# The second FFN product by seven block products for 32 of 44 tiles, between the next part's up-products

## The chip, the cores and the metric

The kernel runs on one core of a Trainium2 chip. The metric is device time in microseconds, the median of several runs. TensorE is the matmul engine, VectorE (DVE), ScalarE (ACT) and GpSimd (POOL) work on rows of 128 partitions, and SyncE (SP) issues most of the data transfers (DMA).

## The reference, cut to what matters

One decoder layer on 256 tokens and 16 meta tokens, width 2048, all in float32. Attention and pooling come first and are not touched. The change lies in the feed-forward part:

```python
def conv_gated_ffn(h, w_up, conv_w, conv_b, w_down):
    T = h.shape[1]
    z = h @ w_up                                   # 2048 -> 2 x 5632
    zp = jnp.pad(z, ((0, 0), (CONV_WIDTH - 1, 0), (0, 0)))
    z = sum(zp[:, j:j + T] * conv_w[j] for j in range(CONV_WIDTH)) + conv_b
    a, g = jnp.split(z, 2, axis=-1)
    return (jax.nn.gelu(a) * g) @ w_down           # 5632 -> 2048
...
    h = layer_norm(ALPHA * h + mix, ln1_g[l], ln1_b[l])
    f = conv_gated_ffn(h, w_up[l], conv_w[l], conv_b[l], w_down[l])
    h = layer_norm(ALPHA * h + f, ln2_g[l], ln2_b[l])
```

## The kernel before

Every float32 product is made of three matmuls. An operand is split into a high part (a copy by ScalarE to the type float32r) and a low part (VectorE subtracts that copy), and high by high, high by low and low by high are added up in PSUM. `fetch` does this for a weight tile of 128 x 2048: one DMA of 1 MB into a raw buffer, and then for each half ScalarE's copy (line 90) and VectorE's subtraction (line 91) into a tile `whl`. There are three raw and three split buffers. All weight tiles are listed in `stream` in the order of their use, and `weights` hands out the next one after `prefetch` has emitted the fetches up to two tiles ahead.

The feed-forward part has 44 tiles of 128 hidden channels, in parts of 16, 12, 12 and 4 (`PARTS`). For each tile there are two up-products (`product`, 48 matmuls of 258 columns: the a half and the g half), a `conv` on each (line 649 on ScalarE, 650 and 651 on VectorE) and a `gate` (gelu on ScalarE, a product on VectorE at line 667, and the split into `gp` at 669 and 670). After the up-products of a part come its down tiles: a tile of the rearranged w_down holds four k-tiles by 512 columns, and each of its k-tiles meets two token halves with three matmuls of 512 columns (lines 717 to 719), 24 matmuls in all. For each of four column groups the sum in PSUM is added to the residual `y2` at line 722. The last part of 4 tiles is done token half by token half at the end (lines 745 to 769), with the second layer norm and the output.

The first four tiles (`FOLDED`) run before the first layer norm's statistics are known and are put right afterwards (`unfold`); meanwhile `normalise` makes the normalised rows. The residual is put into `y2` by 16 VectorE transposes (line 704, four for each of tiles 4 to 7) and 32 DMAs of 64 KB on SyncE's queue (`residual`, line 643, four for each of tiles 8 to 15).

Each engine works through a queue of its own in order. The framework that builds the program settles each queue's order ahead of time by priority (the order of the program) and by which instructions it reckons to be ready, so that an instruction of a later step can stand ahead of one that would have to wait.

Of the kernel before, what the change touches and what calls it, by code (L numbers as in the profile page):

```python
# [31 lines left out]
TOPK = min(256, S // 4)  # L32
FF = 5632
FT = FF // P
PARTS = (16, 12, 12, 4)
FOLDED = 4
MF = 80 + C
NE = NQ + 2
# [6 lines left out]
KW = KA + KB  # L45
STRIP = 400
G_KV, G_POOL, LN1, C_W, C_B, N_COLS = 0, 2, 10, 42, 306, 394


@with_exitstack  # L50
def tile_layer(ctx, tc, xt, w_first, w_proj, w_uk, w_uv, w_pool, w_o, w_up, w_down, cols, rows, rel_bias, onehot, out):
# [8 lines left out]
    def big():  # L60
        return pm.tile([P, 512], F32, tag="mm", name="mm")
# [14 lines left out]
    f0 = d0 = 0  # L76
    for n in PARTS:
        for f in range(f0, f0 + n):
            stream += [w_up[f], w_up[FT + f]]
        stream += [w_down[d] for d in range(d0, d0 + n)]  # L80
        f0, d0 = f0 + n, d0 + n
    spare, last = len(stream) - PARTS[-1], len(stream) - 1
    ready = {}
    state = {"next": 0, "use": 0}

    def fetch(raw, hl, src, c):
        nc.sync.dma_start(raw[:, c], src)
        mid = (c.start + c.stop) // 2
        for c in (slice(c.start, mid), slice(mid, c.stop)):
            nc.scalar.activation(hl[:, 0, c], raw[:, c], AF.Copy)  # L90
            nc.vector.tensor_tensor(hl[:, 1, c], raw[:, c], hl[:, 0, c].bitcast(F32), op=ALU.subtract)  # L91

# [3 lines left out]
    def emit(i):  # L96
        if i in ready:
            return
        if i == last:

            raw = wp.tile([P, 2048], F32, tag="wraw", name="wraw")
            nc.sync.dma_start(raw, stream[i])
            ready[i] = []
            for c in range(0, 2048, 256):
                hl = ring.tile([P, 2, 256], F32R, tag="act", name="whl_r", padded_shape=[P, 2, T])
                nc.scalar.activation(hl[:, 0, :], raw[:, c:c + 256], AF.Copy)
                nc.vector.tensor_tensor(hl[:, 1, :], raw[:, c:c + 256], hl[:, 0, :].bitcast(F32), op=ALU.subtract)
# [7 lines left out]
        fetch(raw, hl, stream[i], slice(0, 2048))  # L115
        ready[i] = hl

    def prefetch(n):
# [435 lines left out]
    output(0)  # L554
    at.close()
    fp = ctx.enter_context(tc.tile_pool(name="ffn", bufs=2))
    acc = fp.tile([P, NQ], F32, name="acc", tag="acc", bufs=1)
    s1 = fp.tile([P, NQ], F32, name="s1", bufs=1)
    s2 = fp.tile([P, NQ], F32, name="s2", bufs=1)
    rs = fp.tile([P, NQ], F32, name="rs", bufs=1)  # L560
    m2 = fp.tile([P, NQ], F32, name="m2", bufs=1)
    folded = []

    def about_k(m):

        yd = y[:, m, Q0:]
        nc.vector.tensor_tensor(yd, yd, acc, op=ALU.subtract)
        sq = fp.tile([P, NQ], F32, name="sq", tag="sq")
        nc.scalar.activation(s2 if m == 0 else sq, yd, AF.Square)
        if m == 1:  # L570
            nc.gpsimd.tensor_tensor(s1, y[:, 0, Q0:], yd, op=ALU.add)
        elif m > 1:
            nc.gpsimd.tensor_tensor(s1, s1, yd, op=ALU.add)
        if m:
            nc.gpsimd.tensor_tensor(s2, s2, sq, op=ALU.add)
        a = fp.tile([P, 2, NE], F32R, name="fold", tag="gp", bufs=18)
# [67 lines left out]

    moves = [(a, b, i) for a in range(4) for b in range(4) for i in range(2)]

    def conv(j, half_, src):
        z = fp.tile([P, S], F32, name="z", tag=f"z{half_}")
        nc.scalar.activation(z, src[:, 2:NQ], AF.Identity, bias=col(C_B, j), scale=col(C_W, 3 * j + 2))  # L649
        nc.vector.scalar_tensor_tensor(z, src[:, 1:NQ - 1], col(C_W, 3 * j + 1), z, op0=ALU.mult, op1=ALU.add)  # L650
        nc.vector.scalar_tensor_tensor(z, src[:, :S], col(C_W, 3 * j), z, op0=ALU.mult, op1=ALU.add)
        return z

    def unfold(ps):
# [5 lines left out]
        w = fp.tile([P, NQ], F32, name="w", tag="acc", bufs=1)  # L660
# [4 lines left out]
    def gate(za, zg):  # L665
        nc.scalar.activation(za, za, AF.Gelu_apprx_tanh)
        nc.vector.tensor_tensor(za, za, zg, op=ALU.mult)
        a = fp.tile([P, 2, S], F32R, name="gp", tag="gp", bufs=18, padded_shape=[P, 2, NE])
        nc.scalar.activation(a[:, 0, :], za, AF.Copy)
        nc.vector.tensor_tensor(a[:, 1, :], za, a[:, 0, :].bitcast(F32), op=ALU.subtract)  # L670
        return a


    f0 = 0
    for part, n in enumerate(PARTS):
        gated = []
        for f in range(f0, f0 + n):
            if part == len(PARTS) - 1 and f - f0 in (0, 2):
                emit((last, spare)[(f - f0) // 2])
            both = []  # L680
            for half_ in range(2):
                hl = weights()
                ps = big()
                if f < FOLDED:
                    k = 0
                    if f + half_ == 0:
                        product(ps[:, :NE], hl, P, folded, 0, NE, k1=7)
                        deviation()
                        product(ps[:, :NE], hl, P, folded, 0, NE, k0=7, k1=14)
                        deviation_rows()  # L690
                        k = 14
                    product(ps[:, :NE], hl, P, folded, 0, NE, k0=k)
                    while len(h_parts) < min(KT, 3 * (2 * f + half_ + 1)):
                        normalise(len(h_parts))
                    both.append(ps)
                else:
                    product(ps[:, :NQ], hl, P, h_parts, 0, NQ)
                    both.append(conv(half_ * FT + f, half_, ps))
            if f < FOLDED:
                both = [conv(half_ * FT + f, half_, unfold(both[half_])) for half_ in range(2)]  # L700
            gated.append(gate(*both))
            if FOLDED <= f < FOLDED + 4:
                for m in range(4 * (f - FOLDED), 4 * (f - FOLDED) + 4):
                    nc.vector.transpose(y[:, m, NM:], y[:, m, NM:])
            if FOLDED + 4 <= f and part == 0:
                for _ in range(4):
                    residual(*moves.pop(0))
        if part + 1 < len(PARTS):
            for c in range(4):
                ps = [big(), big()]  # L710
                for g in range(n // 4):
                    hl = weights()
                    for k in range(4 * g, 4 * g + 4):
                        w = slice(512 * (k - 4 * g), 512 * (k - 4 * g) + 512)
                        for i in range(2):
                            t = slice(i * P, (i + 1) * P)
                            nc.tensor.matmul(ps[i], gated[k][:, 0, t], hl[:, 0, w], start=k == 0, stop=False)  # L717
                            nc.tensor.matmul(ps[i], gated[k][:, 0, t], hl[:, 1, w], start=False, stop=False)  # L718
                            nc.tensor.matmul(ps[i], gated[k][:, 1, t], hl[:, 0, w], start=False, stop=k == n - 1)  # L719
                for i in range(2):  # L720
                    yc = y2[:, i, 512 * c:512 * c + 512]
                    nc.vector.scalar_tensor_tensor(yc, yc, 1.0 if part else ALPHA, ps[i], op0=ALU.mult, op1=ALU.add)
        f0 += n


    gb = []
    for r in range(2):
        for c in range(4):
            t = fp.tile([P, 512], F32, name="gb", tag="gp", bufs=18, padded_shape=[P, 2 * NE])
            nc.gpsimd.dma_start(t, rows[r:r + 1, 512 * c:512 * c + 512].to_broadcast([P, 512]))  # L730
            gb.append(t)
    n = PARTS[-1]
    hls = [weights(ahead=n) for _ in range(n)]
    order = [0, n - 1] + list(range(1, n - 1))
    for i in range(2):
# [98 lines left out]
```

## Time and profile before

| | us |
|---|---|
| median of 3 runs | 1080.12 (1079.86 to 1081.37) |
| the profiled execution | 1081.53 |
| its span, from first to last instruction | 1079.7 |
| TensorE busy | 1064.7 |
| VectorE busy | 712.5 |
| ScalarE busy | 524.9 |
| GpSimd busy | 100.0 |

The mean granted TensorE clock was 0.997 of full speed, and 200.17 MB were moved, at 185 GB/s in the mean. Durations of one instruction are in ns in the groups and in us in the timelines. In a timeline each row is start, duration, engine, line, operation, output from input, count, and in brackets the idle time before it with what ended it. Consecutive instructions of an engine overlap a little, so what an instruction takes from its engine is the time from its start to the next one's start. In the windows the columns are the stretch, its length, the busy time of TensorE's matmuls, its weight loads, VectorE, ScalarE and GpSimd, the granted clock, the DMA engines' busy share and GB/s.

### The profile page before, as it was taken

Reading aid. Unit: us, or ns where it says so; the run is one execution under the profiler, and the core shown is the slowest. Engines: PE = TensorE matmul, PEld = TensorE weight load, DVE = VectorE, ACT = ScalarE, POOL = GpSimd, SP = SyncE. Lnnn points to the kernel's source line nnn. Section 1 sums busy time; section 2 is a strip of 40 time slices with the busy share of each in tenths; the row PEclk is TensorE's granted clock in tenths of the full one; section 3 lists DMA queues with packets and bytes.
Section 4 is the critical chain, followed back from the end, with each engine's and each line's share of the span. In section 5 each row is a group of like instructions: output and inputs, shape, how many; then the busy total and the mean of one; then the engine's idle time right before and its main releaser. Section 6 shows DMA issues by size and latency. Waiting matters only on the chain.

```text
span 1079.7 us, 18694 instructions
## 1 busy us (share of the span) xinstructions
PE 1064.7 (99%) x7770; PEld 1008.5 (93%) x7770; DVE 712.5 (66%) x1083; ACT 524.9 (49%) x828; POOL 100.0 (9%) x131
## 2 busy tenths in 40 slices
PE   9999999999999999999999999999999999999996
PEld 8998999999999999999888999998899999988995
DVE  5879468758879975665454656655556666555757
ACT  6666446645457754454333544543344454434530
POOL 1100013126454100000000000000000000001000
PEclk9999999999999999999999999999999999999998
DMA  8756533444543686665555555555555555557712
GB/s 304 256 171 235 195 138 118 164 168 156 195 157 118 200 259 201 192 203 195 185 180 187 190 178 174 196 178 185 187 212 182 173 192 181 181 187 246 274 43 79
DMA packets 47653, 200.17 MB, mean 185 GB/s; under 512 B 20390, under 2 KB 20816, under 8 KB 25168
## 3 DMA queue, kind: packets, MB, share of 16 engines
q1 hardware_dynamic: 45872, 194.11, 53.5%
q0 software_dynamic: 1120, 3.82, 1.2%
q8 instruction: 61, 1.00, 0.4%
q10 hardware_dynamic: 576, 1.05, 0.3%
q14 instruction: 24, 0.20, 0.1%
HBM read 194.75 MB, written 2.11 MB: 182 GB/s over the span
## 4 chain that ended last, share of the span: by engine, by line
PE 92%; DVE 5%; DMA 2%; ACT 1%; issue 0%; POOL 0%; SPq 0%; ACTq 0%; DVEq 0%; POOLq 0%
PE mm L142 22%; PE mm L141 22%; PE mm L143 21%; PE mm L717 7%; PE mm L718 7%; PE mm L719 7%; DVE whl L91 1%; DMA wraw<-in_w_first 1%; DVE x L632 1%; DVE hp L636 1%; DMA wraw<-in_w_proj 1%; PE at L295 0%; PE mm L747 0%; PE mm L745 0%; PE at L296 0%
## 5 line engine op out<-in xcount | busy, mean ns | idle before, releaser
L91 DVE TENSOR_TENSOR whl<-wraw,whl 128x1024 fp32r<-128x1024 f32 x344 | 421.3, 1250 | 123.1 <-ACT whl L90 121.2
L90 ACT ACTIVATE whl<-wraw 128x1024 fp32r<-128x1024 f32 x344 | 346.7, 1050 | 174.4 <-PE mm L719 120.1
L141 PE MATMUL mm<-hp,whl 128*128 128x258 f32 x1280 | 363.7, 284 | 0.0
L142 PE MATMUL mm<-hp,whl 128*128 128x258 f32 x1280 | 363.3, 284 | 0.0
L143 PE MATMUL mm<-hp,whl 128*128 128x258 f32 x1280 | 361.1, 282 | 0.0
L143 PEld LDWEIGHTS mm<-hp,whl 128*128 128x128 f32 x1280 | 244.3, 191 | 0.0
L142 PEld LDWEIGHTS mm<-hp,whl 128*128 128x128 f32 x1280 | 244.1, 191 | 0.1
L141 PEld LDWEIGHTS mm<-hp,whl 128*128 128x128 f32 x1280 | 241.8, 189 | 0.1
L650 DVE SCALAR_TENSOR_TENSOR z<-mm,cv,z 128x256 f32<-128x256 f32 x80 | 38.7, 484 | 162.6 <-ACT z L649 162.5
L649 ACT ACTIVATE z<-mm,cv 128x256 f32<-128x256 f32 x80 | 45.1, 564 | 200.5 <-PE mm L143 200.4
L717 PE MATMUL mm<-whl,gp 128*128 128x512 f32 x320 | 126.4, 395 | 0.0
L719 PE MATMUL mm<-whl,gp 128*128 128x512 f32 x320 | 126.2, 394 | 0.0
L718 PE MATMUL mm<-whl,gp 128*128 128x512 f32 x320 | 126.2, 394 | 0.0
L141 PE MATMUL mm<-xp,whl 128*128 128x256 f32 (+5 forms) x384 | 111.1, 289 | 0.0
L143 PE MATMUL mm<-xp,whl 128*128 128x256 f32 (+5 forms) x384 | 109.1, 284 | 0.8 <-DVE whl L91 0.8
L142 PE MATMUL mm<-xp,whl 128*128 128x256 f32 (+5 forms) x384 | 109.5, 285 | 0.0
L143 PEld LDWEIGHTS mm<-xp,whl 128*128 128x128 f32 x384 | 72.5, 189 | 1.3 <-DVE whl L91 1.2
L719 PEld LDWEIGHTS mm<-whl,gp 128*128 128x128 f32 x320 | 60.1, 188 | 14.3
L141 PEld LDWEIGHTS mm<-xp,whl 128*128 128x128 f32 x384 | 72.7, 189 | 0.8 <-ACT whl L90 0.2
L717 PEld LDWEIGHTS mm<-whl,gp 128*128 128x128 f32 x320 | 60.2, 188 | 13.9
L718 PEld LDWEIGHTS mm<-whl,gp 128*128 128x128 f32 x320 | 60.1, 188 | 13.9
L142 PEld LDWEIGHTS mm<-xp,whl 128*128 128x128 f32 x384 | 72.3, 188 | 0.8 <-issue 0.5
(266 smaller groups left out, 1397.6 us busy)
## 6 DMA issues: line engine op xcount, KB each, us to landing
wraw<-in_w_up SPq DMA_DIRECT2D x88, 1024.0 KB, 5.0
wraw<-in_w_down SPq DMA_DIRECT2D x44, 1024.0 KB, 4.9
wraw<-in_w_proj SPq DMA_DIRECT2D x24, 1024.0 KB, 5.0
wraw<-in_w_o SPq DMA_DIRECT2D x16, 1024.0 KB, 4.9
wraw<-in_w_first SPq DMA_DIRECT2D x9, 304.0 KB, 6.5
x<-in_xt SPq DMA_DIRECT2D x1, 2176.0 KB, 8.7
y<-x SPq DMA_DIRECT2D x32, 64.0 KB, 5.4
gb<-in_rows POOLq DMA_DIRECT2D x8, 256.0 KB, 6.1
```

Source lines behind the costliest of these rows:

```text
L90: nc.scalar.activation(hl[:, 0, c], raw[:, c], AF.Copy)
L91: nc.vector.tensor_tensor(hl[:, 1, c], raw[:, c], hl[:, 0, c].bitcast(F32), op=ALU.subtract)
L141: nc.tensor.matmul(ps, wh, ah, start=n == 0, stop=False)
L142: nc.tensor.matmul(ps, wh, al, start=False, stop=False)
L143: nc.tensor.matmul(ps, wl, ah, start=False, stop=n == KT - 1)
L632: nc.vector.tensor_tensor(yd, yd, m2, op=ALU.add)
L636: nc.vector.tensor_tensor(a[:, 1, :NQ], yd, a[:, 0, :NQ].bitcast(F32), op=ALU.subtract)
L649: nc.scalar.activation(z, src[:, 2:NQ], AF.Identity, bias=col(C_B, j), scale=col(C_W, 3 * j + 2))
L650: nc.vector.scalar_tensor_tensor(z, src[:, 1:NQ - 1], col(C_W, 3 * j + 1), z, op0=ALU.mult, op1=ALU.add)
L717: nc.tensor.matmul(ps[i], gated[k][:, 0, t], hl[:, 0, w], start=k == 0, stop=False)
L718: nc.tensor.matmul(ps[i], gated[k][:, 0, t], hl[:, 1, w], start=False, stop=False)
L719: nc.tensor.matmul(ps[i], gated[k][:, 1, t], hl[:, 0, w], start=False, stop=k == n - 1)
```

## The change

`PARTS` becomes (8, 8, 8, 8, 8, 4). For the first four parts (`FAST`) the second product is made by seven block products in place of eight, by a scheme of Strassen's kind. k-tiles are taken in pairs, so that the gated activations of a pair and 256 tokens form 2 x 2 blocks of 128 x 128 (token half by k-tile), and a tile of the rearranged w_down holds 2 x 2 blocks of 128 x 512 (k-tile by column group c or c + 2).

- Left operands: `forms` makes four block sums of the activations with four GpSimd additions of 128 x 128 for each pair, and splits seven blocks (three splits of 256 columns and one of 128).
- Right operands: each tile is fetched twice. Kind "A" makes one block difference of 512 columns on VectorE ahead of the split and is used for four products, 12 matmuls. Kind "B" makes three block sums, one after the other, splits three of the four blocks, and is used for three products, 9 matmuls.
- Results: the seven sums stay in the four buffers of the pool `pa` over the four pairs of a part. At the end of A, ScalarE copies two of them to `u` and `v`, VectorE adds three to `y2`, and two DMAs on GpSimd's queue add `u` and `v` to blocks of `y2`. At the end of B, VectorE makes two sums and adds one, and three DMAs add the rest.
- Order: `ffn_plan` writes out the order. The down items of a part (16: two column groups, A then B, four pairs each) alternate one by one with the 16 up-products of the next part. The fifth part's down tiles run as before, after its up-products and the fourth part's down items, and the last four tiles are as before.
- The transposes of the residual move to tiles 4 and 5 (eight each), the 32 moves to tiles 6 to 9 (eight each). The pool of `gp` has 16 buffers in place of 18.

```diff
-PARTS = (16, 12, 12, 4)
+PARTS = (8, 8, 8, 8, 8, 4)
+FAST = 4
...
+def ffn_plan():
+    plan, f0 = [], 0
+    for part, n in enumerate(PARTS[:-1]):
+        ups = [("up", f, half_) for f in range(f0, f0 + n) for half_ in range(2)]
+        downs = []
+        if 0 < part <= FAST:
+            m = PARTS[part - 1] // 2
+            downs = [(kind, part - 1, c, j) for c in range(2) for kind in "AB" for j in range(m)]
+        while ups or downs:
+            plan += ups[:1] + downs[:1]
+            ups, downs = ups[1:], downs[1:]
+        if part >= FAST:
+            plan += [("down", part, c, g) for c in range(4) for g in range(n // 4)]
+        f0 += n
+    return plan + [("up", f, half_) for f in range(f0, FT) for half_ in range(2)]
...
+    def fetch(raw, hl, src, kind=None):
+        nc.sync.dma_start(raw, src)
+        b11, b12, b21, b22 = (raw[:, c:c + 512] for c in range(0, 2048, 512))
+        cuts = (0, 1024, 2048)
+        if kind == "A":
+            nc.vector.tensor_tensor(b12, b12, b11, op=ALU.subtract)
+        if kind == "B":
+            nc.vector.tensor_tensor(b12, b22, b12, op=ALU.subtract)
+            nc.vector.tensor_tensor(b11, b12, b11, op=ALU.add)
+            nc.vector.tensor_tensor(b21, b21, b11, op=ALU.subtract)
+            cuts = (0, 1024, 1536)
+        for c in (slice(a, b) for a, b in zip(cuts, cuts[1:])):
             nc.scalar.activation(hl[:, 0, c], raw[:, c], AF.Copy)
             nc.vector.tensor_tensor(hl[:, 1, c], raw[:, c], hl[:, 0, c].bitcast(F32), op=ALU.subtract)
...
+    def two_parts(a, src):
+        nc.scalar.activation(a[:, 0], src, AF.Copy)
+        nc.vector.tensor_tensor(a[:, 1], src, a[:, 0].bitcast(F32), op=ALU.subtract)
         return a
...
+    def forms(r, j):
+        a11, a21, a12, a22 = r[:, 0, :P], r[:, 0, P:], r[:, 1, :P], r[:, 1, P:]
+        s = fp.tile([P, 4 * P], F32, name="forms", tag="acc", bufs=1).rearrange("p (a b) -> p a b", b=P)
+        nc.gpsimd.tensor_tensor(s[:, 0], a21, a22, op=ALU.add)
+        nc.gpsimd.tensor_tensor(s[:, 2], s[:, 0], a11, op=ALU.subtract)
+        nc.gpsimd.tensor_tensor(s[:, 1], a12, s[:, 2], op=ALU.subtract)
+        nc.gpsimd.tensor_tensor(s[:, 3], a11, a21, op=ALU.subtract)
+        left = two_parts(slot(), r[:, :, :P])
+        mid = two_parts(slot(), s[:, :2])
...
+        right = two_parts(right[:, :, :2 * P].rearrange("p a (b c) -> p a b c", c=P), s[:, 2:])
...
+        two_parts(held["lone"][:, :, j % 2], a22)
...
+    def seven(kind, part, c, j):
+        hl = weights()
+        n = PARTS[part] // 2
+        names = (("P2", 2), ("P3", 3), ("P1", 0), ("P5", 1)) if kind == "A" else (("P7", 1), ("P6", 0), ("P4", 2))
+        if j == 0:
+            for name, _ in names:
+                held[name] = small()
+        for name, w in names:
+            a, i = pairs[part][j][name]
+            ps, w = held[name], slice(512 * w, 512 * w + 512)
+            nc.tensor.matmul(ps, a[:, 0, i], hl[:, 0, w], start=j == 0, stop=False)
+            nc.tensor.matmul(ps, a[:, 0, i], hl[:, 1, w], start=False, stop=False)
+            nc.tensor.matmul(ps, a[:, 1, i], hl[:, 0, w], start=False, stop=j == n - 1)
+        if j < n - 1:
+            return
...
+        if kind == "A":
...
+            nc.scalar.activation(held["u"], held["P1"], AF.Copy)
...
+            nc.scalar.activation(held["v"], held["P5"], AF.Copy)
+            add(c11, held["P2"])
+            add(c12, held["P3"])
+            add(c22, held["v"])
+            nc.gpsimd.dma_start(c11, held["u"], accum_op=ALU.add)
+            nc.gpsimd.dma_start(c12, held["v"], accum_op=ALU.add)
+        else:
+            u, v = held["u"], held["v"]
+            nc.vector.tensor_tensor(u, u, held["P6"], op=ALU.add)
+            nc.vector.tensor_tensor(v, u, held["P7"], op=ALU.add)
+            add(c21, held["P4"])
+            nc.gpsimd.dma_start(c12, u, accum_op=ALU.add)
+            nc.gpsimd.dma_start(c21, v, accum_op=ALU.add)
+            nc.gpsimd.dma_start(c22, v, accum_op=ALU.add)
...
+        if f in (FOLDED, FOLDED + 1):
+            for m in range(8 * (f - FOLDED), 8 * (f - FOLDED) + 8):
+                nc.vector.transpose(y[:, m, NM:], y[:, m, NM:])
+        if FOLDED + 2 <= f < FOLDED + 6:
+            for _ in range(8):
+                residual(*moves.pop(0))
```

More of the change, by code (lines that the diff above doesn't have):

```diff
@@ L114, in emit @@
             raw, hl = weight_tiles()
-        fetch(raw, hl, stream[i], slice(0, 2048))
+        fetch(raw, hl, stream[i], kinds.get(i))
         ready[i] = hl
@@ L575, in about_k @@
             nc.gpsimd.tensor_tensor(s2, s2, sq, op=ALU.add)
[L576 removed]
+        a = fp.tile([P, 2, NE], F32R, name="fold", tag="gp", bufs=16)
         gb = cv[:, LN1 + 2 * m:LN1 + 2 * m + 2]
@@ new lines, in tile_layer @@
+        gate(*both)
+        if part >= FAST:
+            a = fp.tile([P, 2, NE], F32R, name="gp", tag="gp", bufs=16)
+            gated.append(two_parts(a[:, :, :S], both[0]))
+        elif f % 2:
+            todo.append((part, pair))
+        while todo and f + 1 >= FOLDED:
+            p, r = todo.pop(0)
+            pairs[p].append(forms(r, len(pairs[p])))
+        if f in (FOLDED, FOLDED + 1):
+            for m in range(8 * (f - FOLDED), 8 * (f - FOLDED) + 8):
+                nc.vector.transpose(y[:, m, NM:], y[:, m, NM:])
```

167 lines of the change are left out of this document (95 added, 72 removed).

## The prediction

> **What bounds the kernel now.** I read the page of the profile first: the busy shares and the chain that ended last.
>
> ```profile
> span 1079.7 us, 18694 instructions
> PE 1064.7 (99%) x7770; PEld 1008.5 (93%) x7770; DVE 712.5 (66%) x1083; ACT 524.9 (49%) x828; POOL 100.0 (9%) x131
> ...
> PE 92%; DVE 5%; DMA 2%; ACT 1%; issue 0%; POOL 0%; SPq 0%; ACTq 0%; DVEq 0%; POOLq 0%
> ```
>
> TensorE is busy for 99% of the span and makes 92% of the chain, so a matmul that goes is time that goes, as long as the others keep up. VectorE is second, with 66%. What one weight tile costs TensorE is read from the timeline of the SyncE queue, since each fetch waits for a buffer that is freed once per tile.
>
> ```profile
> 451.45 0.33 SPq L87 DMA_DIRECT2D wraw<-in_w_up  x1
> ...
> 474.60 84.47 SPq L87 DMA_DIRECT2D wraw<-in_w_down  x16
> 564.32 133.16 SPq L87 DMA_DIRECT2D wraw<-in_w_up  x24
> ```
>
> An issue takes 0.33 us. 24 up tiles make 23 intervals in 133.16 - 0.33, 5.78 us each, for 48 matmuls. 16 down tiles make 15 intervals in 84.47 - 0.33, 5.61 us each, for 24 matmuls of 512 columns: 0.234 us a matmul.
>
> **The change part by part.** *Removed from TensorE.* Two k-tiles times two token halves times four column groups are 16 block products of 3 matmuls, 48 for a pair of tiles. Seven products replace eight, so 14 x 3 = 42 are left. 16 pairs (32 tiles) save 96 matmuls x 0.234 = 22.4 us, and that is all the change can give. Nothing else on TensorE changes: its up-products, the remaining down tiles and the end are the same.
>
> *Added: fetches.* Kinds A and B read the same tile of w_down, once each, so 32 fetches become 64, and each has its own split. What a fetch costs the DMA engines comes from the windows, and from the issues:
>
> ```profile
> 0.00:30.00 30.00, 27.48 (x193) 24.90 (x194) 18.76 (x43) 20.12 (x44) 3.56 (x12) 1.00 0.86 300
> 580.00:690.00 110.00, 110.00 (x880) 108.34 (x879) 67.06 (x91) 51.94 (x72) 0.00 (x0) 1.00 0.54 182
> ...
> wraw<-in_w_up SPq DMA_DIRECT2D x88, 1024.0 KB, 5.0
> ...
> out<-y ACTq DMA_DIRECT2D x4, 256.0 KB, 2.5
> ```
>
> The last two figures are DMA share and GB/s. In the up stretch a tile of 5.78 us uses 0.54 of the engines, so 3.1 us of all of them. Up tile and down tile then alternate. Kind A has 12 matmuls, B has 9, so a pair (one up, one down tile) takes TensorE 5.78 + 2.80 = 8.58 us with A, 5.78 + 2.10 = 7.88 with B, on average 8.23; 64 such pairs are 527 us. The weights take 6.2 of 8.23 us of the DMA engines, 75%. Ten accumulating transfers of 256 KB a part come on top. The trace has none: below they cost nothing (they hide in the 25% left), above three times the 2.5 us of a plain output, 7.5 us each, 75 us in a part of 16 pairs x 8.23 = 132 us, which would not fit. I take 1.6 us, twice what 256 KB take at the 300 GB/s of the first window, nearest in being a full queue: 16 us, 12% of a part, 87% in all. A fetch still has time: its raw buffer is freed about one pair ahead, 8 us, against 5.0 to landing.
>
> *Added: VectorE.* This is the term that decides. The groups of VectorE, and its timeline in the up stretch:
>
> ```profile
> L91 DVE TENSOR_TENSOR whl<-wraw,whl 128x1024 fp32r<-128x1024 f32 x344 | 421.3, 1250 | 123.1 <-ACT whl L90 121.2 <-PE at L454 0.8 <-PE at L499 0.8
> ...
> L670 DVE TENSOR_TENSOR gp<-z,gp 128x256 fp32r<-128x256 f32 x44 | 19.0, 432 | 0.6 <-ACT gp L669 0.5
> ...
> L722 DVE SCALAR_TENSOR_TENSOR y<-y,mm 128x512 f32<-128x512 f32 x24 | 16.4, 688 | 15.7 <-PE mm L719 15.6
> ```
>
> ```profile
> 600.89 0.48 DVE L650 SCALAR_TENSOR_TENSOR z<-mm,cv,z 128x256 f32<-128x256 f32 x1 [2.48 <-ACT z L649]
> 601.41 0.48 DVE L651 SCALAR_TENSOR_TENSOR z<-mm,cv,z 128x256 f32<-128x256 f32 x1
> 601.84 1.23 DVE L91 TENSOR_TENSOR whl<-wraw,whl 128x1024 fp32r<-128x1024 f32 x1
> 602.98 0.42 DVE L667 TENSOR_TENSOR z<-z 128x256 f32<-128x256 f32 x1
> 603.32 1.22 DVE L91 TENSOR_TENSOR whl<-wraw,whl 128x1024 fp32r<-128x1024 f32 x1
> ```
>
> What counts is from start to start: 1.14 us for 1024 columns (601.84 to 602.98), 0.34 for 256 (to 603.32), 0.95 for a conv (600.89 to 601.84). On that line 512 columns are 0.61 (0.69 alone, L722) and 128 are 0.21, estimates. Per pair:
> an up split 2.28; a conv 0.95; half a gate 0.17; a quarter of the forms (three splits of 256, one of 128, for four up tiles) 0.31; a quarter of the sums (three of 512 for each four down tiles) 0.46: together 4.17. A adds one difference and a whole split, 0.61 + 2.28 = 2.89; B three block sums and three quarters of a split, 1.83 + 1.14 + 0.61 = 3.58. So A needs 7.06 and B 7.75. ScalarE has less to do:
>
> ```profile
> L90 ACT ACTIVATE whl<-wraw 128x1024 fp32r<-128x1024 f32 x344 | 346.7, 1050 | 174.4 <-PE mm L719 120.1 <-issue 29.1 <-PE mm L143 21.2
> L649 ACT ACTIVATE z<-mm,cv 128x256 f32<-128x256 f32 x80 | 45.1, 564 | 200.5 <-PE mm L143 200.4
> ...
> L666 ACT ACTIVATE z<-z 128x256 f32<-128x256 f32 x44 | 17.8, 405 | 3.1 <-DVE z L651 3.1
> ```
>
> Four halves of 1.05 us, a conv of 0.56 and a share of gate, forms and sums make some 5.5 of 8.23 us a pair.
>
> The forms also put four GpSimd additions of 128 columns beside this, per four pairs. What such an addition does to VectorE stands in the timeline at 304 us:
>
> ```profile
> 304.75 1.61 DVE L91 TENSOR_TENSOR whl<-wraw,whl 128x1024 fp32r<-128x1024 f32 x1 [0.26 <-ACT whl L90]
> ...
> 307.18 1.21 DVE L91 TENSOR_TENSOR whl<-wraw,whl 128x1024 fp32r<-128x1024 f32 x1
> ```
>
> ```profile
> 304.64 0.64 POOL L573 TENSOR_TENSOR s<-s,x 128x258 f32<-128x258 f32 x1 [3.46 <-DVE x L567]
> 305.24 1.72 POOL L575 TENSOR_TENSOR s<-s,sq 128x258 f32<-128x258 f32 x1
> ```
>
> The split goes from 1.21 to 1.61 us, and the addition from 0.64 to 1.72. Bounds for one addition are 0 and 0.4 us of VectorE; for half as many columns I take 0.3, so 0.3 a pair: A 7.36, B 8.05, mean 7.7 against TensorE's 8.23. VectorE would be at 94%, and in a run of four B pairs over TensorE by 0.17 a pair, 0.7 us in a run. Tiles are fetched two ahead, and a split is started when the product before the last has ended: that leaves about 4 us before TensorE waits, and the A pairs win it back (7.36 against 8.58).
>
> By the Trainium skill (SBUF — State Buffer, Who interferes with whom) a VectorE instruction with two SBUF inputs and a GpSimd instruction that reads SBUF exclude each other for the whole instruction, whichever began first. It speaks against this change, whose block sums, splits and forms are all of these kinds. The addition's 1.72 against 0.64 us agrees, the split's 0.40 is less than the 0.64 that the rule asks. By the row the sum is the one below; by the rule it is that of the rival of GpSimd's hold.
>
> What is not packing but waiting: the split's second half cannot start before ScalarE's copy, and ScalarE's copy now waits for VectorE's block sums. When VectorE has no slack, does it keep that full? The windows of the stretch where it has none:
>
> ```profile
> 318.00:336.00 18.00, 18.00 (x151) 18.00 (x151) 17.42 (x27) 11.41 (x22) 16.12 (x18) 1.00 0.21 69
> 336.00:354.00 18.00, 17.30 (x144) 17.09 (x144) 18.00 (x41) 17.56 (x34) 1.96 (x2) 1.00 0.47 156
> ```
>
> 17.42 and 18.00 of 18 us: there other work fills the waits, though ScalarE ran ahead then, as it can't before a block sum. An unfilled wait would cost 0.35 (B: 1.05 less the third sum) to 1.05 us (A) a pair. I take a quarter of all waits as unfilled (a quarter of the 1.76 us worked out under the rivals), 0.44 a pair: mean 8.15, just under 8.23, with the B runs 4 x (8.49 - 7.88) = 2.4 us late against 4 us of lead. Where sums and forms fall together the lead will not do: I take 1 us for each of the eight B runs, 8 us (from 0 to 2.4 + 1.8 for the sums in each, 34 us).
>
> *Moved.* The transposes (16, now in two tiles' time rather than four), and the 32 residual moves, eight a tile rather than four, from tile 6. Their rows:
>
> ```profile
> y<-x SPq DMA_DIRECT2D x32, 64.0 KB, 5.4
> ...
> 394.59 0.68 SPq L643 DMA_DIRECT2D y<-x  x1
> ```
>
> Eight issues take 8 x 0.68 = 5.4 us of the SyncE queue in 11.6 us of a tile; the next fetch stands behind them, but SyncE runs about a pair ahead. The first sums need all moves landed (5.4 us); the last are queued ahead of the fourth A product's fetches, so 0 to 5 us once, and I take 1. The forms of the first four tiles and the transposes are put on the stretch where VectorE is full: 2 us (0 to 5). The forms' wait on GpSimd holds ScalarE's queue, with the next splits behind it; that is in the 8 us. The sums that the GpSimd queue now does by DMA cost no engine time but the issues; the last of them land 10 us before the down tiles' sums read them, two tiles of 5.61.
>
> *Sum.* The profiled execution took 1081.5 us (span 1079.7): 1081.5 - 22.4 + 8 + 1 + 2 = 1070.1. It is 1.4 us above the median of the runs, 1080.1, so 1069 is to be expected of a median.
>
> **The rivals.** *VectorE and ScalarE in turns become the bound: slower.* If nothing fills the waits, a B pair is conv 0.95, two dependent block sums 1.4 (0.69 each), ScalarE's copy 1.05, splits 1.14 + 0.61, the up split 2.28, 7.41 us; an A pair 0.95 + 0.69 + 1.05 + 2.28 + 2.28 = 7.25. Add the gate with ScalarE's gelu (0.41 + 0.42 for every second up tile, 0.42), the sums (0.46), and the forms in turns with GpSimd, four additions at about 0.9 (between 0.64 and 1.72, for fewer columns) and four copies and splits, 5 us in four pairs, 1.25: 9.46 a pair. Against 8.23 that is 64 x 1.23 = 79 us. The saving is lost where the mean passes 8.23 + 22.4/64 = 8.58, that is where 0.88 of the 1.76 us between packed (7.70) and turn by turn (9.46) stay unfilled, half. At 0.7 of it, 8.93, the time is 1080.1 - 22.4 + 45 + 3 = 1106, the 3 being the single costs of the sum. For it: the block sums ahead of the copies, and the 1.72 us additions. Against it: the 98% of the packed stretch. Chance 0.28.
>
> *GpSimd's additions hold VectorE for all of their time.* Then each costs it up to 0.64 us, a pair 0.34 more than I took, and the mean of 8.15 becomes 8.49: 64 x (8.49 - 8.23) = 17 us in place of the 8, 1080.1 - 22.4 + 17 + 3 = 1078, and no change that could be told. For it: the 1.72 us. Against it: the 0.40. Chance 0.08.
>
> *Data late.* If an accumulating transfer costs 5 us, the engines stand at 75% + 38%: a part of 132 us would grow by 13%, 17 us. With 5 to 17 us in each of four parts the time is 1078 to 1126. For it: three raw buffers only, and 5.0 us to landing in 8. Against it: the 0.86 at 300 GB/s that the first window sustained. Chance 0.08.
>
> *Full gain.* VectorE's lead always does: 1080.1 - 22.4 + 0 to 3, 1058 to 1061. It is the forecast's lower neighbour, chance 0.14.
>
> **How the numbers follow.** Forecast (1061 to 1077, middle 1069) 0.42, full gain 0.14, turns 0.28, GpSimd's hold 0.08, data late 0.08. 0.2% is 2.2 us, about what a measurement of this kernel can tell from no change. Faster: 0.42 + 0.14 = 0.56. Same: GpSimd's hold, 0.08, and 0.02 for data late at its mild end, 0.10. Slower: the turns and the rest of data late, 0.34. The range runs from 1058, the full gain, to 1098, where the turns have 8.8 a pair; above it lies some 0.15.
>
> **What would show it.** TensorE with 96 matmuls fewer of 512 columns; pairs of 8.2 to 8.4 us from start to start in parts two to five; VectorE over 90% busy there; TensorE waiting for splits in B runs only. Wrong if the mean pair is 8.6 or more, if VectorE idles on ScalarE's copies in these parts, if GpSimd's additions take over 1 us each and ScalarE's forms wait for them, or if ScalarE's copies wait for DMA.

## The result and the profile after

The changed kernel takes 1078.06 us (median of 16 runs, 1076.46 to 1080.19) against 1080.11 us before (16 runs beside them), a ratio of 0.9981 (95% interval 0.9974 to 0.9989). It is 2 us faster, where 11 were forecast. The profiled execution took 1079.12 us, 2.4 less than the one before.

From the page of the profile after: span, busy time of each engine, the granted clock in 40 slices, and the chain that ended last.

```profile
span 1077.0 us, 19083 instructions
PE 1050.5 (98%) x7674; PEld 996.5 (93%) x7674; DVE 875.3 (81%) x1339; ACT 592.4 (55%) x940; POOL 179.6 (17%) x235
...
PEclk9999999999999999889999999999999999999998
...
PE 85%; DVE 8%; DMA 2%; ACT 2%; POOL 1%; issue 1%; SPq 0%; DVEq 0%; ACTq 0%; POOLq 0%
```

TensorE has its 96 matmuls fewer (7770 to 7674), but its busy time fell by 14.2 us only, and in two slices in the middle of the span the clock is lowered. The steady part is as forecast, as SyncE's timeline and the windows show (columns of the windows: stretch, length, busy time of TensorE's matmuls, its weight loads, VectorE, ScalarE, GpSimd, granted clock, DMA share, GB/s):

```profile
503.54 0.33 SPq L111 DMA_DIRECT2D wraw<-in_w_up  x1
...
569.46 0.33 SPq L111 DMA_DIRECT2D wraw<-in_w_up  x1
```

```profile
372.00:400.00 28.00, 25.06 (x193) 24.64 (x193) 23.21 (x38) 17.68 (x31) 6.62 (x11) 0.94 0.78 220
400.00:435.00 35.00, 33.55 (x256) 32.28 (x255) 20.12 (x30) 13.99 (x21) 3.29 (x5) 1.00 0.71 201
435.00:450.00 15.00, 13.31 (x68) 11.31 (x69) 11.70 (x13) 8.79 (x10) 0.00 (x0) 0.77 0.56 137
450.00:466.00 16.00, 10.14 (x61) 8.59 (x60) 9.70 (x18) 6.88 (x12) 3.27 (x5) 0.80 0.64 208
466.00:500.00 34.00, 34.00 (x243) 32.06 (x242) 30.79 (x43) 19.09 (x26) 5.74 (x7) 0.99 0.77 285
632.00:666.00 34.00, 34.00 (x242) 32.02 (x241) 31.51 (x43) 19.44 (x27) 5.65 (x8) 1.00 0.87 283
```

Eight pairs take 569.46 - 503.54 = 65.92 us, 8.24 a pair (8.23 forecast), TensorE is busy without a break there, and VectorE for 30.8 to 31.5 of 34 us. What is lost is lost between 372 and 466 us, the hand-over from the first part to the mixed order. TensorE's waits say for what (in total, times, the longest):

```profile
PE at L745 <- ACT whl L124: 8.9, 2, 5.8
PE mm L175 <- ACT whl L124: 2.2, 1, 2.2
PE mm L177 <- DVE whl L125: 1.1, 2, 0.8
...
PE at L745 <- DVE u L767: 0.8, 1, 0.8
```

2.2 and 0.8 us at 377 us (gap 1), 3.1 at 434 (gap 2) and 5.8 at 457 (gap 3), 11.9 in all; only the 0.8 for `u` lies in the steady part, right behind a B run. With each gap comes a stretch in which TensorE is granted half its clock:

```profile
382.00:384.00 2.00, 2.00 (x11) 2.00 (x11) 2.00 (x4) 2.00 (x4) 0.27 (x1) 0.50 0.88 213
...
460.00:462.00 2.00, 0.00 (x0) 0.00 (x0) 1.93 (x4) 0.73 (x2) 1.17 (x2) 0.50 0.67 119
```

The five windows from 372 to 500 us hold 28 x 0.06 + 15 x 0.23 + 16 x 0.20 + 34 x 0.01 = 8.7 us of missing clock. Not all of it costs time: as the second row here shows, part of a half-clock stretch can lie inside the gap itself. In windows of 0.25 us that part is 0.5 us in gap 2 and 1.6 us in gap 3, so the clock costs 8.7 - 2.1 = 6.6 us. Gaps and clock together are 11.9 + 6.6 = 18.5 us. The account: 22.4 saved, 18.5 + 0.8 lost, 3.1 less; the profiled execution has 2.4 less, so the sum closes within 0.7 us.

Gap 1 in ScalarE's timeline:

```profile
373.03 0.42 ACT L706 ACTIVATE gp<-forms 128x256 fp32r<-128x256 f32 x1 [2.36 <-POOL forms L722]
...
376.46 0.42 ACT L706 ACTIVATE right<-forms 128x256 fp32r<-128x256 f32 x1 [0.84 <-POOL forms L721]
...
377.77 1.99 ACT L124 ACTIVATE whl<-wraw 128x1024 fp32r<-128x1024 f32 x2
```

Both first pairs have their forms behind tile 3. ScalarE's queue waits for GpSimd's additions, and the weight copies (L124) that TensorE needs stand behind. Gaps 2 and 3 look different (ScalarE, then VectorE):

```profile
433.59 0.56 ACT L683 ACTIVATE za<-mm,cv 128x256 f32<-128x256 f32 x1 [8.01 <-PE mm L177]
...
435.55 4.83 ACT L124 ACTIVATE whl<-wraw 128x1024 fp32r<-128x1024 f32 x5
...
457.01 0.56 ACT L683 ACTIVATE za<-mm,cv 128x256 f32<-128x256 f32 x1 [3.96 <-PE mm L177]
...
461.69 3.47 ACT L124 ACTIVATE whl<-wraw 128x1024 fp32r<-128x1024 f32 x4 [0.96 <-DVE wraw L120]
```

```profile
434.19 0.48 DVE L684 SCALAR_TENSOR_TENSOR za<-mm,cv,za 128x256 f32<-128x256 f32 x1 [7.11 <-ACT za L683]
...
435.11 0.68 DVE L116 TENSOR_TENSOR wraw<-wraw 128x512 f32<-128x512 f32 x1
```

ScalarE stands still for 8.01 us in front of a conv, which needs an up-product that TensorE is still working on; five weight copies are queued behind it. VectorE stands still for 7.11 us in front of the same conv's second step, with the block difference of the next A tile (line 116) behind that. When the up-product ends, TensorE's next block product needs those copies and waits. SyncE's queue in the same stretch:

```profile
409.15 6.84 SPq L677 DMA_DIRECT2D y<-x  x8
...
424.20 0.33 SPq L111 DMA_DIRECT2D wraw<-in_w_down  x1
439.01 0.33 SPq L111 DMA_DIRECT2D wraw<-in_w_up  x1
439.39 7.51 SPq L677 DMA_DIRECT2D y<-x  x8
447.01 0.55 SPq L111 DMA_DIRECT2D wraw<-in_w_down  x1
```

Eight moves take 6.8 to 7.5 us of it, and nothing is fetched from 424.2 to 439.0, since all raw buffers hold uncopied tiles. Two readings were open here: fetches are bodily held behind the moves, or the order of ScalarE's queue, which is settled ahead of time, is a bad one.

The trace itself speaks for the order. The A tile of gap 2 was fetched at 418.27, 2.3 us after the moves before it had ended, and landed 4.7 us later, at 423.0; its block difference began only at 435.11. The B tile of gap 3 was fetched at 447.01, right behind eight moves, but it landed 5.3 us later, at 452.3, while TensorE stopped at 457.0; in between VectorE and ScalarE were idle for some 4 us, each in front of the next conv.

### The profile page after: what moved, and what is told of

Same layout as the page of the kernel before. It is cut to its first block, busy times and chain, and to the rows that moved or that the text cites. A ratio compares the mean times of both kernels' runs of the same rounds, so it can differ in the third digit from the quotient of the medians.

```text
span 1077.0 us, 19083 instructions
## 1 busy us (share of the span) xinstructions
PE 1050.5 (98%) x7674; PEld 996.5 (93%) x7674; DVE 875.3 (81%) x1339; ACT 592.4 (55%) x940; POOL 179.6 (17%) x235
## 4 chain that ended last, share of the span: by engine, by line
PE 85%; DVE 8%; DMA 2%; ACT 2%; POOL 1%; issue 1%; SPq 0%; DVEq 0%; ACTq 0%; POOLq 0%
PE mm L175 20%; PE mm L176 20%; PE mm L177 20%; PE at L745 4%; PE at L746 4%; PE at L747 4%; DVE whl L125 3%; PE mm L792 1%; PE mm L793 1%; PE mm L794 1%; DMA wraw<-in_w_up 1%; ACT whl L124 1%; DMA wraw<-in_w_down 1%; DVE hp L670 1%; DVE x L666 1%
## 5 line engine op out<-in xcount | busy, mean ns | idle before, releaser
L125 DVE TENSOR_TENSOR whl<-wraw,whl 128x1024 fp32r<-128x1024 f32 (+1 forms) x408 | 478.3, 1207 | 55.6 <-ACT whl L124 54.0
L124 ACT ACTIVATE whl<-wraw 128x1024 fp32r<-128x1024 f32 (+1 forms) x408 | 396.7, 1016 | 147.8 <-DVE wraw L116 36.0
L683 ACT ACTIVATE z<-mm,cv 128x256 f32<-128x256 f32 x40 | 22.6, 565 | 86.6 <-PE mm L177 86.6
L745 PE MATMUL at<-whl,gp 128*128 128x512 f32 x160 | 64.5, 405 | 3.9 <-ACT whl L124 3.1
L746 PE MATMUL at<-whl,gp 128*128 128x512 f32 x160 | 64.1, 401 | 0.0
L747 PE MATMUL at<-whl,gp 128*128 128x512 f32 x160 | 63.8, 399 | 0.0
L683 ACT ACTIVATE za<-mm,cv 128x256 f32<-128x256 f32 x40 | 22.5, 563 | 71.8 <-PE mm L177 71.8
L723 POOL TENSOR_TENSOR forms<-za 128x128 f32<-128x128 f32 x16 | 15.2, 951 | 173.7 <-DVE za L701 171.9
L684 DVE SCALAR_TENSOR_TENSOR z<-mm,cv,z 128x256 f32<-128x256 f32 x40 | 19.3, 482 | 27.6 <-ACT z L683 27.6
L745 PEld LDWEIGHTS at<-whl,gp 128*128 128x128 f32 x160 | 30.7, 192 | 10.3 <-ACT whl L124 3.3
```

The source lines that it names most:

```text
L723: nc.gpsimd.tensor_tensor(s[:, 3], a11, a21, op=ALU.subtract)
L745: nc.tensor.matmul(ps, a[:, 0, i], hl[:, 0, w], start=j == 0, stop=False)
L746: nc.tensor.matmul(ps, a[:, 0, i], hl[:, 1, w], start=False, stop=False)
L747: nc.tensor.matmul(ps, a[:, 1, i], hl[:, 0, w], start=False, stop=j == n - 1)
```

## Experiments

All ratios are to the kernel before, on the same chip. The theory from the traces: gap 1 belongs to the forms, gaps 2 and 3 to the residual moves. Against it stood the prediction's own rivals (VectorE and ScalarE in turns, GpSimd's hold, data late).

**e1_no_moves.** The moves are left out and `y2` is zeroed, so the residual is missing.

```diff
-        if FOLDED + 2 <= f < FOLDED + 6:
-            for _ in range(8):
-                residual(*moves.pop(0))
+        if f == FOLDED + 2:
+            nc.gpsimd.memset(y2, 0.0)
```

> Leaves out the 32 residual moves; y2 is set to zero by GpSimd at tile 6 instead, so the residual is missing from the sums. Theory (hand-over): seven products save their whole 22.4 us, and some 20 us are lost again between 372 and 466 us of the changed kernel, in three TensorE gaps and the halved clock behind them. The moves, eight a tile, cause the second and third gap: 3.1 + 5.8 us and two stretches of 6.8 us at half clock, 15.7 us together. Expected 1062 us (1059 to 1066), the first gap still there. Rival 1 (VectorE and ScalarE in turns are the bound all along): 1078 us. Rival 2 (the gaps belong to the start of the alternation of up and down tiles, whatever the moves do): 1076 to 1078 us.

Measured 1063.89 us, 0.9849 (0.9834 to 0.9864). Its windows:

```profile
372.00:400.00 28.00, 25.08 (x194) 24.66 (x193) 23.18 (x38) 17.75 (x31) 6.52 (x10) 0.94 0.58 200
400.00:466.00 66.00, 66.00 (x488) 63.07 (x487) 54.73 (x76) 36.89 (x52) 9.03 (x11) 1.00 0.67 230
```

From 400 to 466 us TensorE has no gap; the first window is that of the change, 25.08 against 25.06 us busy at 0.94. So 14.2 of the 18.5 us come with the moves (gaps 2 and 3 with their half clock are 13.6 in the account above).

**e2_forms_apart.** The first two pairs' forms are made behind two tiles instead of one.

```diff
-        while todo and f + 1 >= FOLDED:
+        if todo and f + 1 >= FOLDED:
```

> One pair's forms a tile at most, so the first two pairs' forms come behind tiles 3 and 4 and not both behind tile 3; nothing else changes. Theory (hand-over): the first gap (2.2 + 0.8 us, and 3.4 us at half clock) comes of ScalarE's queue, where the weight copies stand behind forms that wait for GpSimd; it goes, 4.7 us: 1073.4 us (1071 to 1076), the other two gaps unchanged. Rival 1 (in turns): 1078 us. Rival 2 (VectorE is full in that stretch anyway, so the gap only shifts): 1077 to 1079 us.

Measured 1074.68 us, 0.9949 (0.9934 to 0.9964). TensorE's waits:

```profile
PE at L745 <- ACT whl L124: 8.9, 2, 5.8
...
PE mm L175 <- ACT whl L124: 0.4, 1, 0.4
```

Gap 1 shrinks from 2.2 to 0.4 us with no half clock behind it, and gaps 2 and 3 stay. It is the other part of the loss, 3.4 us. Together e1 and e2 explain 17.6 of the 18.5 us.

**e3_moves_pool.** The same moves, the same bytes, on GpSimd's queue.

```diff
-        nc.sync.dma_start(to, y[src, :, t:t + 32])
+        nc.gpsimd.dma_start(to, y[src, :, t:t + 32])
```

> The 32 moves are issued on GpSimd's queue instead of SyncE's; the same bytes move at the same tiles. Theory (hand-over, by the order of the queues): the weight fetches no longer stand behind eight moves, and the order settled ahead has the weight copies in front of the convs again; the second and third gap go: 1063 us (1060 to 1067). Rival (by the load of the DMA engines, which the 512 packets of 128 B in each move fill): the gaps stay, 1074 to 1079 us. A third possibility: descriptors on GpSimd hold the forms, 1068 to 1074 us.

Measured 1064.6 us, 0.9861 (0.984 to 0.9883): almost as good as without moves. A window where the moves run:

```profile
384.00:402.00 18.00, 18.00 (x152) 18.00 (x151) 11.41 (x17) 9.56 (x15) 11.20 (x17) 1.00 1.03 247
```

The DMA engines are full (1.03) and TensorE does not wait. So it is not the moves' bytes or packets; it is their place on SyncE's queue. And the order of ScalarE's queue is another one: four copies stand ahead of the conv that has five behind it in the change:

```profile
426.83 4.10 ACT L124 ACTIVATE whl<-wraw 128x1024 fp32r<-128x1024 f32 x4 [1.78 <-issue]
432.60 0.57 ACT L683 ACTIVATE za<-mm,cv 128x256 f32<-128x256 f32 x1 [1.66 <-PE mm L177]
```

**e4_turn_pe, e5_turn_forms, e6_before_turn.** The residual is turned by 32 TensorE transposes and eight ScalarE copies, behind tiles 4 to 7, so that VectorE's transposes and all moves go; e5 has e2's edit as well; e6 is the kernel before with the same turning, as a control.

```diff
-            for m in range(8 * (f - FOLDED), 8 * (f - FOLDED) + 8):
-                nc.vector.transpose(y[:, m, NM:], y[:, m, NM:])
...
+            for i in range(2):
+                ps = small()
+                for q in range(4):
+                    t = NM + i * P
+                    nc.tensor.transpose(ps[:, q * P:(q + 1) * P], y[:, 4 * c + q, t:t + P], ident)
+                nc.scalar.activation(y2[:, i, 512 * c:512 * c + 512], ps, AF.Copy)
```

> The residual is turned by 32 TensorE transposes of 128x128 at tiles 4 to 7, copied to y2 by eight ScalarE copies of 512 columns; the 16 VectorE transposes and the 32 moves go. Theory (hand-over): as without moves, 1062 us, plus 32 x 0.1 to 0.3 us of TensorE: 1065 to 1071 us, 1067 the likeliest. Rival 1 (in turns): 1078 us plus the transposes, 1081 to 1088. Rival 2 (start of the alternation): the same, 1080 to 1087.

> Both mends at once: the residual turned by TensorE (32 transposes at tiles 4 to 7) and the first two pairs' forms a tile apart. Theory (hand-over): what is left is the saving of 22.4 us less 32 x 0.1 us of transposes and less a short gap at 377 us: 1058 to 1062 us, at most 1 to 2 us below the version with the turn alone (1062.8), where the first gap had shrunk to 0.6 us already. Rival (something else still costs in the alternation): no change, 1062.8 us.

> The kernel before with the residual turned by TensorE in the same way, in place of its 16 VectorE transposes and 32 moves. It tells how much of the 17 us that the turn won in the changed kernel belongs to the seven products. Theory (hand-over): the kernel before has no gap at its moves, so the turn only adds 32 x 0.1 us or takes as much from the VectorE-bound stretch: 1078 to 1084 us. Rival (the turn is worth its 15 us in any kernel, since the moves always cost): 1064 to 1068 us.

Measured: e4 1062.8 us, 0.9844 (0.9828 to 0.9861); e5 1061.32 us, 0.9826 (0.9812 to 0.9841), the fastest of all; e6 1083.32 us, 1.0029 (1.0018 to 1.0039). The turning itself costs 3.3 us (1080.01 for the kernel before beside it), and with it on both sides seven products win 1083.32 - 1061.32 = 22.0 us. The saving of 22.4 us is there in full once the hand-over has no gaps.

**e7_two_more.** How much room has VectorE in the steady part? e5 with two cancelling operations of 512 columns more for every A and B tile, reckoned at 1.22 us a pair (the part for A is shown).

```diff
         if kind == "A":
             nc.vector.tensor_tensor(b12, b12, b11, op=ALU.subtract)
+            nc.vector.tensor_tensor(b12, b12, b11, op=ALU.add)
+            nc.vector.tensor_tensor(b12, b12, b11, op=ALU.subtract)
```

> On top of both mends, each fetch of kind A and B makes two more VectorE operations of 512 columns that cancel each other (subtract and add again, one after the other), 1.22 us more a pair. It puts VectorE over TensorE, so that the period of a pair reads off VectorE's own need. If the waits between the engines are filled by other work (packed, 7.7 us a pair before): 7.70 + 1.22 = 8.92 against 8.23, 64 x 0.69 = 44 us more, 1104 us. With GpSimd's additions holding VectorE for their whole time (8.04): 9.26, 66 us more, 1126. Turn by turn (9.46 and two dependent operations of 0.69): 10.84, 167 us more, 1227.

Measured 1126.35 us, 1.0426 (1.0402 to 1.0451). Eight pairs of it, between two fetches of up tiles:

```profile
598.65:673.78 75.13, 70.23 (x470) 63.25 (x468) 70.00 (x99) 39.17 (x55) 11.04 (x14) 0.98 0.72 242
```

A pair takes 75.13 / 8 = 9.39 us, of which VectorE is busy for 70.00 / 8 = 8.75 and idle for 0.64. Without the dose that is 7.53 busy and 0.64 of waits, 8.17 us, against TensorE's 8.23. In the B tiles the added operations, each of which needs the one before, start 0.72 us apart (604.12, 604.84 and 605.57), so the dose may be as much as 1.44 us and the need without it 7.95. It fits neither end of the forecast, 1104 or 1227: VectorE is the bound here and is not packed to the full, and far from turn by turn. That the time falls on the number of GpSimd's hold is no sign for that rival, as the rows of VectorE show below.

**e8_blocks.** e5 without the alternation: the up-products of a part, then its 16 block items in a row.

```diff
-        while ups or downs:
-            plan += ups[:1] + downs[:1]
-            ups, downs = ups[1:], downs[1:]
...
+        plan += ups + downs
```

> On top of both mends, the alternation is undone: a part's up-products first, then its 16 down items in a row. Nothing else changes. TensorE's need of 16 down items is 39 us; VectorE's, packed, is per column group 4 x 2.89 + 4 x 3.58 + 1.83 x 2 = 29.5 us, so 59 us a part. Packed: 4 x 20 = 79 us more, some 1140 us; turn by turn (about 4.0 to 4.2 a fetch and the sums): 139 us more, 1200 us. If the alternation is not needed: 1060 to 1065 us.

Measured 1158.99 us, 1.0729 (1.0707 to 1.075), 97.7 more than e5. A stretch of 60 us with block items, and TensorE's first wait:

```profile
580.00:640.00 60.00, 49.99 (x235) 37.65 (x235) 52.22 (x66) 30.88 (x36) 6.91 (x8) 0.89 0.92 289
```

```profile
PE at L743 <- ACT whl L122: 42.5, 27, 4.1
```

The scheme lives on its order: alone, a block item leaves TensorE waiting for copies 27 times, and the clock falls to 0.89.

**e9_moves_fine.** Back to the change, to settle why the moves hurt on SyncE's queue: four moves ahead of each up-product instead of eight behind each tile. The theory then: shorter clumps let ScalarE's queue be filled in a good order.

```diff
+        if FOLDED + 2 <= f <= FOLDED + 5:
+            for _ in range(4):
+                residual(*moves.pop(0))
...
-        if FOLDED + 2 <= f < FOLDED + 6:
-            for _ in range(8):
-                residual(*moves.pop(0))
```

> The 32 moves stay on SyncE's queue, at the same tiles 6 to 9, but are emitted four ahead of each up-product instead of eight behind each tile. The bytes, the queue and the pace are the same; what changes is the order settled ahead: on ScalarE's queue each weight copy now stands between the convs, where the changed kernel has two convs in a row in front of four weight copies. By the order: the second gap goes and the third shrinks, 1063 to 1069 us, 1066 the likeliest. By SyncE's queue (fetches behind moves): the gaps stay or change little, 1074 to 1080 us.

Measured 1077.68 us, 0.997 (0.9958 to 0.9981): a miss. TensorE's waits:

```profile
PE mm L175 <- ACT whl L124: 8.4, 4, 4.5
PE mm L177 <- DVE whl L125: 3.7, 7, 0.8
```

The two long gaps became several shorter ones. ScalarE's queue still had convs ahead of the copies, so this run could not tell the order from the queue.

**e10_pool_apart.** e3 and e2 together, with no turning on TensorE.

> Moves on GpSimd's queue (1064.6 us alone) and the first two pairs' forms a tile apart (3.4 to 4.5 us alone). Theory (hand-over): the parts add up and no gap over 1 us is left before the steady part: 1060 us (1058 to 1062), as good as the turn on TensorE with the forms apart (1061.3), which pays about 3 us of transposes. Rival (the first gap moves elsewhere when the moves' descriptors share GpSimd's queue with the forms): 1063 to 1066 us.

Measured 1062.3 us, 0.9829 (0.9812 to 0.9845): two lines of the code give all but 1 us of what e5 has. That is between the two forecasts, and short gaps of up to 1.0 us are left in it.

**e11_sixteen, e12_eleven.** These tell the order from the queue. All moves stay on SyncE's queue, in longer clumps, chosen by the order in which ScalarE's queue comes out of the build.

```diff
-        if FOLDED + 2 <= f < FOLDED + 6:
-            for _ in range(8):
+        if 6 <= f < 8:
+            for _ in range(16):
```

> Edit: the 32 residual moves stay on SyncE's queue, all bytes and all issues as in the change, but sixteen stand behind tile 6 and sixteen behind tile 7, rather than eight behind each of tiles 6 to 9. In this build ScalarE's queue, from the second block product on, is filled in the order of the steady part (a conv, then the copies of the next tiles), while in the change and in the run with four moves ahead of each up-product it holds up to three convs, gates and sums ahead of the copies. Theory of the order (the gaps come from copies that stand behind instructions which wait for TensorE): the two later gaps of 3.1 and 5.8 us and their half-clock stretches go, the first gap (2.2 + 0.8 us, 3.4 us at half clock) stays, one short gap more at most behind the moves: 1064 to 1068 us. Theory of the queue (fetches held bodily behind small issues): sixteen issues of 0.68 us are 11 us in a row, twice the clump of the change, so each of the two clumps leaves TensorE without a split for some 5 us, with half clock behind: 1076 to 1084 us.

```diff
...
+        if 6 <= f < 9:
+            for _ in range(11):
+                moves and residual(*moves.pop(0))
```

> Edit: as the last, with eleven, eleven and ten moves behind tiles 6, 7 and 8. Here ScalarE's queue again holds two convs with their gates, the two copies of the sums and four forms ahead of copies around the first block products. Theory of the order: gaps of 3 to 6 us between 400 and 470 us of the span with half clock behind, 1072 to 1080 us, although the clumps are shorter than with sixteen. Theory of the queue: clumps of 7.5 us, a little longer than the change's 5.4 to 6.8, so about the time of the change, less than with sixteen: 1074 to 1080 us; sixteen would be the slower of the two.

Measured: e11 1067.56 us, 0.988 (0.9864 to 0.9897); e12 1071.68 us, 0.9921 (0.9906 to 0.9936). SyncE and ScalarE of e11, then SyncE and ScalarE of e12:

```profile
396.42 15.63 SPq L677 DMA_DIRECT2D y<-x  x16
```

```profile
437.75 0.57 ACT L683 ACTIVATE za<-mm,cv 128x256 f32<-128x256 f32 x1 [3.75 <-PE mm L177]
438.21 2.00 ACT L124 ACTIVATE whl<-wraw 128x1024 fp32r<-128x1024 f32 x2
```

```profile
409.21 10.76 SPq L677 DMA_DIRECT2D y<-x  x10
421.95 0.33 SPq L111 DMA_DIRECT2D wraw<-in_w_down  x1
```

```profile
435.26 0.56 ACT L683 ACTIVATE za<-mm,cv 128x256 f32<-128x256 f32 x1 [8.01 <-PE mm L177]
...
437.22 4.83 ACT L124 ACTIVATE whl<-wraw 128x1024 fp32r<-128x1024 f32 x5
```

In e11 the queue is blocked by moves for 15.63 us in a row, against 9.22 at most in the change, and gaps 2 and 3 are gone; one of 1.36 and 0.75 us stands behind the clump. In e12 the clumps are shorter, the pattern of the change is back to the hundredth (a conv that waits 8.01 us, five copies behind it), and so is gap 2 with its 3.1 us; gap 3 is not, and the time is just below the 1072 to 1080 us expected. e11 lies in the range of the theory of the order, 1064 to 1068, and that of the queue had sixteen as the slower of the two; it is the faster.

The two runs differ in one more thing: in e11 the last move ends at 412.05, before the first block product at 416.2. So the times alone could also mean that only clumps beside block products hurt. The rows of e12 exclude that for gap 2: the last move ends at 419.97, the tile of the gap is fetched at 421.95 and lands 5.0 us later, at 427.0, and TensorE stops at 435.2, 15 us after the last move, while ScalarE stands in front of the conv. The order of ScalarE's queue, with VectorE's to match, makes gaps 2 and 3. The moves have their part in it, since that order comes out another way with their place (e3, e11, e12). That the build reckons with the delay of the fetches behind them is the likely reason; it was not looked at by itself. The time for which the moves hold the fetches bodily costs little beside that: at most the 3 us between e11 and e3, its gap of 2.1 us and the half clock behind. Even that gap may be the order's in part, since its copies stand behind a conv and a gate.

## Why the prediction was right and wrong

- *Removed*, 22.4 us: right. 96 matmuls are gone, and e5 against e6 measures 22.0.
- Pairs of 8.23 us: right, 8.24 measured; e5's gain shows that no part of the steady stretch is lost.
- Fetches: right that data is not late. The DMA share in the steady part is 0.77 to 0.87 (0.87 forecast), and e3 had 1.03 with TensorE at work. From 500 to 920 us VectorE and ScalarE wait for a fetch 16 times, 2.7 us at the longest, and TensorE never. What an accumulating transfer costs the DMA engines was not measured by itself (twice 256 KB at 300 GB/s is 1.7 us, not 1.6); from issue to landing it took 3.5 us for `u` and 7.4 us for `v`, the medians.
- VectorE at 94% with a quarter of the waits unfilled: near. It is at 31.51 of 34 us, 93%, and by e7 it needs 7.95 to 8.17 us a pair with its waits, where 7.70 and 0.44 made 8.15. GpSimd's additions cost VectorE less than the 0.3 us a pair that I took:

```profile
L125 DVE TENSOR_TENSOR whl<-wraw,whl 128x1024 fp32r<-128x1024 f32 x28 | 33.5, 1232 | 0.8 <-ACT whl L124 0.7
...
L707 DVE TENSOR_TENSOR gp<-za,gp 128x256 fp32r<-128x256 f32 x2 | 1.3, 655 | 0.0
L707 DVE TENSOR_TENSOR gp<-forms,gp 128x256 fp32r<-128x256 f32 x2 | 0.9, 426 | 2.1 <-ACT gp L706 2.1
```

  These are VectorE's groups from 500 to 566 us (busy, mean ns of one). A split takes 1232 ns against 1250 before. In four pairs one operation of 256 columns and two splits meet the additions: 655 - 426 = 0.23 us, and 2.62 - 2.36 = 0.26 us by the rows in the last section, an estimate of 0.1 us a pair.
- The B runs, 8 us: too much. TensorE waits once, 0.8 us, right behind a run; the lead did what the *full gain* rival said. These 7 us too many hid part of the error that follows.
- *Moved*, 1 + 2 us: this is the step that failed. It came to 18.5 us by the account of the trace and 17.6 by the runs: 14.2 for the moves (e1) in place of 1, and 3.4 for the forms (e2) in place of 2. I priced the moves as a delay of the next fetch ("SyncE runs about a pair ahead") and found it small; e11 says that this much was nearly right, at most 3 us for a longer clump. What I did not price is that the moves' place on SyncE's queue changes the order of ScalarE's and VectorE's queues, where copies and block differences then stand behind convs that wait for TensorE. The forms' hold on ScalarE's queue I had seen, and put into the 8 us of the steady part; it struck where two pairs' forms come at once, in gap 1. There a sign of being wrong that I had named came true: the first of the four additions took 1034 ns in the mean, and ScalarE waited 2.36 us for forms.
- Not in the sum at all: the clock. 6.6 of the 18.5 us are the half clock that comes with the gaps.

The rivals: turns is ruled out by the steady part, where a pair takes 8.24 us and not 9.46. GpSimd's hold gave 1078, the number that came, but by luck: the steady pairs are not at 8.49. Data late is ruled out by e3. Full gain, 1058 to 1061, is what the change has in it, and e5 reaches it but for its 3 us of turning.

## What to carry to other kernels

When work is moved, ask not only whether its queue has time for it, but what it does to the order of the other engines' queues: find in the timeline the instruction that an engine stands in front of and what is queued behind it. A change of steady state pays at its hand-over, so cost the first round by itself, with the forms, sums and moves that all begin there. And when TensorE is the bound, a gap of a few us can cost up to twice its length: behind gap 2, 3.1 us long, the half clock cost 2.9 us more.

## What the runs showed of the hardware

- A half-clock stretch came behind a gap of 2.2 us and one of 0.8 half a microsecond later (0.94 over 28 us: 28 x 0.06 / 0.5 = 3.4 us long). In e11 one came behind 1.36 and 0.75 us, the only gaps in that stretch. Behind gap 1 of e2, 0.4 us with 0.7 shortly after, there was none. The window of e11:

```profile
400.00:435.00 35.00, 32.89 (x235) 31.26 (x235) 24.19 (x33) 18.17 (x24) 3.31 (x5) 0.95 0.78 245
```

  The Trainium skill (TensorE: Matmul & The Clock Gate, Why this matters for your kernels) asks for no gaps over about 3 us. Here less was enough, where two short gaps stood close together.
- GpSimd's additions give way more than VectorE does. Two groups of GpSimd in the change (busy, mean ns of one), and a moment of the steady part on GpSimd and on VectorE:

```profile
L720 POOL TENSOR_TENSOR forms<-za 128x128 f32<-128x128 f32 x16 | 16.5, 1034 | 120.2 <-DVE za L701 120.1
...
L722 POOL TENSOR_TENSOR forms<-za,forms 128x128 f32<-128x128 f32 x16 | 7.7, 480 | 1.3
```

```profile
511.08 1.30 POOL L723 TENSOR_TENSOR forms<-za 128x128 f32<-128x128 f32 x1 [11.45 <-DVE za L701]
```

```profile
510.85 2.62 DVE L125 TENSOR_TENSOR whl<-wraw,whl 128x1024 fp32r<-128x1024 f32 x2
```

```profile
446.31 2.36 DVE L125 TENSOR_TENSOR whl<-wraw,whl 128x1024 fp32r<-128x1024 f32 x2 [2.10 <-ACT whl L124]
```

  The last row has two splits with no addition beside them. An addition that falls beside splits takes 1.30 us rather than some 0.48, so 0.8 more, and the two splits 2.62 - 2.36 = 0.26 more. The Trainium skill (SBUF — State Buffer, Who interferes with whom) has whoever issues first hold the other off, and says that the order of issue decides who blocks: the splits began first here, and the runs agree in that. The rival priced the other order.
- A move of 64 KB takes 0.85 to 1.15 us of SyncE's queue in clumps (6.84 to 9.22 us for 8, 15.63 for 16), where 0.68 was read from a single one before.
